# Experts' weights in 2 MB pieces, in places of 16 KB per partition

## The chip, the cores and the metric

The kernel runs on one core of a Trainium2 chip. The metric is the device time of one execution in microseconds (us). Three runs of the kernel before took 2021.32, 2018.51 and 2013.82 us, median 2018.51 us.

## The reference, cut to what matters

Two transformer blocks over 512 tokens of width 1024, all in float32. The first block is a mixer (projections, convolutions, pooling), a LayerNorm, a mixture of experts and a gated side branch ("ple"), then another LayerNorm. The second block has attention, a recurrent part and a dense feed-forward. The change touches the experts:

```
logits = h @ router_w + router_b            # 512 tokens, 32 experts
gates, idx = softmax(top_k(logits, 4))      # every token goes to 4 experts
gu  = x_e @ w_gate_up[e] + b_gate_up[e]     # 1024 -> 2048, tokens of expert e
act = (clip(up) + 1) * min(gate, 7) * sigmoid(1.702 * gate)
y_e = act @ w_down[e] + b_down[e]           # 1024 -> 1024
out[token] += gate * y_e
```

Each of the 32 experts has 8 MB of w_gate_up and 4 MB of w_down, 384 MB in all, and every byte of it is read once.

## The kernel before, in words

The order of the work on each engine is the order of the Python code; a DMA or an instruction waits only for the data it needs and for the space it writes.

The mixer streams its weights through a `Stream`: half-places of 4 KB per partition hold raw weights, ScalarE (line 179) and VectorE (line 188) split each into a high and a low part in the `kh` and `rh` tiles. When the stream is through, these tiles become places for the experts' weights.

The experts run one after the other, 32 of them. Expert 0 is fixed in the code; the order of the others is found at run time, so that 13 "large" ones (up to 96 tokens) and 19 "small" ones (up to 64) alternate: for i = 1 to 6 large, small, large, small, large, small, then large, small, large, small, small over and over. Per step i the code runs `gate_up(i)`, for i = 0, 2, 4, 6 also `gate1` (a quarter of the side branch: 24 matmuls on lines 268 to 270), and then `down(i - 1)`.

Weights come through `Chunks`. A chunk is 1 MB: 128 partitions with 8 KB each. An expert has 8 chunks for `gate_up` and 4 for `down`. The list `free` holds places; `loads` takes the first fitting one and lets SyncE's queue (SP, line 233) issue the DMA into it; `get` hands the next chunk to the matmuls (lines 1137 and 1210); `release(n)` gives the n oldest places back. A small expert releases after each chunk. A large one first runs the matmuls for its first 64 tokens on four chunks, then those for the other 32 tokens on the same four (lines 1143 and 1217), and releases all four then. SP works its queue in order, and at most eight of its DMAs are under way: the ninth waits until the first has landed.

Places before: three chunks are loaded into `rw` tiles ahead of a run-time loop (`overflow`, which runs zero times here but holds all engines until its count is known). After it three places are added (`kh` twice, `zw`), and during expert 0 `kw0`, `kw1` and the last `rw` come free: nine places of 1 MB. At i = 6, when the side branch no longer needs its tiles, nine more are given. The last chunks go only into places that the second block doesn't need early (`tail`, `last`).

GpSimd's queue (POOL) carries the other traffic: per expert a `gather` of its tokens' rows and, in `finish`, a scatter that adds its results to `acc`; in expert 0 also eight accumulating DMAs of 256 KB (`ple_bias`, lines 962 and 968), which read the tiles z0 to z3 and others. `activate(0)` overwrites z0, z1 and z2 (line 1154 is ScalarE's sigmoid into z2), so it waits for the first three of them.

Of the kernel before, what the change touches and what calls it, by code (L numbers as in the profile page):

```python
# [21 lines left out]
T = 512  # L22
D = 1024
# [69 lines left out]
def prepare(i):  # L93
# [25 lines left out]
    o["w_gate_up"] = a["w_gate_up"][0]  # L119
    o["b_gate_up"] = a["b_gate_up"][0]  # L120

    w = a["w_down"][0].reshape(NE, 4, 2, 128, D).transpose(0, 1, 3, 2, 4)
    o["w_down"] = np.ascontiguousarray(w).reshape(NE, 4, 128, 2 * D)
# [89 lines left out]
class Chunks:  # L213


    def __init__(self, nc):
        self.nc, self.free, self.plan, self.raw = nc, [], [], {}
        self.nl = self.pos = 0
        self.limit, self.hold = 0, False
        self.tail, self.last = 0, ()  # L220
# [5 lines left out]
    def loads(self):  # L226
        while not self.hold and self.nl < min(self.limit, len(self.plan)):
            ok = [i for i, (n, p) in enumerate(self.free) if n in self.last or
                  self.nl < len(self.plan) - self.tail * (2 if n[0] == "k" else 1)]
            if not ok:  # L230
                return
            self.raw[self.nl] = place = self.free.pop(ok[0])
            self.nc.sync.dma_start(place[1], self.plan[self.nl]())
            self.nl += 1

    def get(self):
        self.loads()
        self.pos += 1
        return self.raw[self.pos - 1][1]

    def release(self, n):

        for i in sorted(self.raw)[:n]:
            self.free.append(self.raw.pop(i))
        self.loads()
# [3 lines left out]
def kernel(ctx: ExitStack, tc: tile.TileContext, h, out, dbg=None):  # L249
# [47 lines left out]
    kw = [keep.tile([128, 2048], F32, name=f"kw{i}") for i in range(2)]  # L297
    made = {}

    def kh(i, when):  # L300
        if (i, when) not in made:
            made[i, when] = keep.tile([128, 2, 1024], F32R, tag=f"kh{i}", name="kh")
        return two(made[i, when])
# [31 lines left out]
    with ExitStack() as first:  # L335
# [12 lines left out]
        rw_ = [ring.tile([128, 2048], F32, name=f"rw{i}") for i in range(4)]  # L348
        rh = ring.tile([128, 2, 1024], F32R, tag="rh", name="rh")
        whole = {("k", i): w for i, w in enumerate(kw)} | {("r", i): w for i, w in enumerate(rw_)}  # L350
        parts_ = {n: halves(w) for n, w in whole.items()}
        st = Stream(nc, [p for n in (("k", 0), ("r", 0), ("k", 1), ("r", 1), ("r", 2), ("r", 3)) for p in parts_[n]],
                    [L(kh, i, 1) for i in range(5)] + [lambda: two(rh)])
# [16 lines left out]
        xh = [slot(f"s{j}", [128, 4, T], F32R) for j in range(2)]  # L370
        xl = [slot(f"s{2 + j}", [128, 4, T], F32R) for j in range(2)]
# [48 lines left out]
        def plan_gu(i):  # L420
            for k in range(8):
                mo.plan.append(lambda k=k: h["w_gate_up"][expert(i), 128 * k:128 * k + 128].rearrange("a p c -> (a p) c"))

        def plan_d(i):
            for k in range(4):
                mo.plan.append(lambda k=k: h["w_down"][expert(i), k].rearrange("a p c -> (a p) c"))
# [6 lines left out]
        mo.limit = 8  # L433
        mo.tail, mo.last = 8, {("r", i) for i in range(4)} | {"rh", "zw", "s1", "s3"}
        given = set()

        def spare():

            for n, w in whole.items():
                a = halves(w)  # L440
# [256 lines left out]
        hTh = [slot(f"s{j}", [128, 4, T], F32R) for j in range(2)]  # L697
        hTl = [slot(f"s{2 + j}", [128, 4, T], F32R) for j in range(2)]
# [410 lines left out]
        kh_of = lambda i: (f"kh{i}", keep.tile([128, 2048], F32, tag=f"kh{i}", name="kw"))  # L1109
        kh_free = [i for i in range(5) if i not in gates_at]  # L1110
        assert 5 in gates_at and len(kh_free) == 2
# [6 lines left out]
        def gate_up(i, pre={}, post={}):  # L1118
# [10 lines left out]
            w, n0 = [], 4 if b else 1  # L1129
            for c in range(8):  # L1130
# [49 lines left out]
        def turn_act(i):  # L1180
            n = CAP if large(i) else CAPS
            if i < NE - 2:
                AT[i] = t = slot(f"y{6 + i % 2}", [128, 4, 2 * n])
            else:
                AT[i] = t = (zs(3) if i % 2 else slot("s2", [128, 512])).rearrange("p (c s) -> p c s", c=4)
# [11 lines left out]
        def down(i, pre={}, post={}):  # L1197
# [3 lines left out]
            w, n0 = [], 4 if b else 1  # L1201
            for c in range(4):
# [9 lines left out]
                if (c + 1) % n0 == 0:  # L1212
# [6 lines left out]
                    mo.release(n0)  # L1219
# [23 lines left out]
        def overflow():  # L1243
# [3 lines left out]
            with tc.For_i(0, nx, 1) as j:  # L1247
# [23 lines left out]
                s3 = keep.tile([128, 2048], F32, tag=f"kh{kh_free[0]}", name="s3")  # L1271
# [10 lines left out]
                def load_gu(k, c0):  # L1282
                    t = keep.tile([128, 4, 512], F32, tag=f"kh{kh_free[1]}", name="wx")
                    src = h["w_gate_up"][ds(ev, 1)].rearrange("a (k p) c -> p (a k) c", p=128)
                    nc.sync.dma_start(t, src[:, 4 * k:4 * k + 4, c0:c0 + 512])
                    return t

                def load_d(k, c0):
                    t = keep.tile([128, 4, 512], F32, tag=f"kh{kh_free[1]}", name="wx")
                    for q in range(2):  # L1290
                        src = h["w_down"][ds(ev, 1), 2 * k + q].rearrange("a p (j c) -> p (a j) c", j=2)
                        nc.sync.dma_start(t[:, 2 * q:2 * q + 2], src[:, :, c0:c0 + 512])
                    return t
# [3 lines left out]
                for hf in range(2):  # L1297
                    o = [tbank(), tbank()]
                    for g in range(2):
# [3 lines left out]
                        for k in range(8):  # L1303
                            if k % 4 == 0:
                                w = load_gu(k // 4, c0)
                            P.matmul(o[g][:CAP], x32[:, k], w[:, k % 4], start=False, stop=k == 7)
                    turn32(swiglu(o[0][:CAP], o[1][:CAP], z3, gate[-1][:CAP]), a32[:, 4 * hf:4 * hf + 4], 4)
                dn = [tbank(), tbank()]
                for n in range(2):
                    for k in range(8):  # L1310
                        if k % 4 == 0:
                            w = load_d(k // 4, 512 * n)
                        P.matmul(dn[n][:CAP], a32[:, k], w[:, k % 4], start=k == 0, stop=k == 7)
# [7 lines left out]
        mo.limit = 12 * NE  # L1321
        mo.give(*[kh_of(i) for i in kh_free], ("zw", work.tile([128, 2304], F32, tag="zw", name="zw")[:, 0:2048]))
# [23 lines left out]
        for i in range(NE):  # L1346
# [38 lines left out]
        ys = slot("s0", [128, 2, D], F32R)  # L1385
# [601 lines left out]
```

## Time and profile before

| | us |
|---|---|
| median of 3 runs | 2018.51 |
| the profiled execution | 2018.47 |
| its span | 2016.7 |
| TensorE (PE) busy | 1890.4 (94%) |
| VectorE (DVE) busy | 768.8 (38%) |
| ScalarE (ACT) busy | 463.5 (23%) |

The profile is one execution. Times in its views count from the span's start; 1.8 us of the execution lie outside the span. In a row with "x8" eight instructions are merged. The experts run from about 232 to 1319 us; before them lies the mixer, behind them the second block.

### The profile page before, as it was taken

Reading aid. Unit: us, or ns where it says so; the run is one execution under the profiler, and the core shown is the slowest. Engines: PE = TensorE matmul, PEld = TensorE weight load, DVE = VectorE, ACT = ScalarE, POOL = GpSimd, SP = SyncE. Lnnn points to the kernel's source line nnn. Section 1 sums busy time; section 2 is a strip of 40 time slices with the busy share of each in tenths; the row PEclk is TensorE's granted clock in tenths of the full one; section 3 lists DMA queues with packets and bytes.
Section 4 is the critical chain, followed back from the end, with each engine's and each line's share of the span. In section 5 each row is a group of like instructions: output and inputs, shape, how many; then the busy total and the mean of one; then the engine's idle time right before and its main releaser. Section 6 shows DMA issues by size and latency. Waiting matters only on the chain.

```text
span 2016.7 us, 24301 instructions
## 1 busy us (share of the span) xinstructions
PE 1890.4 (94%) x9434; PEld 1063.2 (53%) x9434; DVE 768.8 (38%) x1517; ACT 463.5 (23%) x811; POOL 110.8 (5%) x125
## 2 busy tenths in 40 slices
PE   8999899999998998998998898889999899999998
PEld 7777533333332332332332232258886588888886
DVE  7967721222121221222121111175665653333454
ACT  4333310101010101010101010232226742222342
POOL 0012200000000000000000000100000000000000
PEclk9999899999999999999999999999999899999999
DMA  7225499999999999999999999923220214333331
GB/s 293 83 81 201 172 355 400 396 400 401 392 399 404 399 401 393 408 391 406 396 406 395 407 392 409 379 68 113 63 63 27 74 58 131 94 95 99 100 94 42
DMA packets 97942, 518.17 MB, mean 257 GB/s; under 512 B 11082, under 2 KB 11098, under 8 KB 48544
## 3 DMA queue, kind: packets, MB, share of 16 engines
q1 hardware_dynamic: 85120, 479.17, 61.1%
q0 software_dynamic: 11376, 35.56, 6.6%
q10 hardware_dynamic: 1328, 1.85, 0.3%
q8 instruction: 76, 1.25, 0.2%
q14 instruction: 42, 0.34, 0.1%
HBM read 496.48 MB, written 20.05 MB: 256 GB/s over the span
## 4 chain that ended last, share of the span: by engine, by line
PE 47%; DMA 36%; DVE 3%; ACT 2%; issue 1%; POOL 0%; SPq 0%; DVEq 0%; ACTq 0%
DMA rw<-in_w_gate_up_dram 13%; PE mm L268 9%; PE mm L270 9%; PE mm L269 9%; DMA kw<-in_w_down_dram 7%; PE mm L1137 6%; PE mm L1210 4%; DMA s<-in_w_down_dram 4%; DMA kw<-in_w_gate_up_dram 4%; DMA zz<-in_w_gate_up_dram 4%; DMA s<-in_w_gate_up_dram 3%; PE mm L1143 3%; PE tr L1608 1%; PE tr L1030 1%; DMA acc<-z 1%; PE mm L1217 1%
## 5 line engine op out<-in xcount | busy, mean ns | idle before, releaser
L1137 PE MATMUL mm<-rw,y 128*64 128x512 f32 x768 | 183.3, 602 | 18.0 <-DMA rw<-in_w_gate_up_dram 17.7
L188 DVE TENSOR_TENSOR kh<-kw,kh 128x1024 fp32r<-128x1024 f32 (+1 forms) x116 | 139.4, 1209 | 153.3 <-ACT kh L179 153.1
L1137 PE MATMUL mm<-kw,y 128*64 128x512 f32 x688 | 167.2, 608 | 22.6 <-DMA kw<-in_w_gate_up_dram 22.2
L1154 ACT ACTIVATE z<-z 128x512 f32<-128x512 f32 (+1 forms) x45 | 28.3, 629 | 661.3 <-DVE z L1153 650.4
L179 ACT CAST kh<-kw 128x1024 fp32r<-128x1024 f32 (+1 forms) x116 | 119.9, 1040 | 252.2 <-PE mm L269 170.3
L270 PE MATMUL mm<-vh,kh 128*128 128x512 f32 (+2 forms) x368 | 140.6, 382 | 0.1
L268 PE MATMUL mm<-vh,kh 128*128 128x512 f32 (+2 forms) x368 | 140.6, 382 | 0.0
L269 PE MATMUL mm<-vl,kh 128*128 128x512 f32 (+2 forms) x368 | 140.5, 382 | 0.0
L1193 DVE COPY y<-tr 128x512 f32<-128x512 f32 (+1 forms) x43 | 25.1, 608 | 267.5 <-PE tr L1191 259.0
L1210 PE MATMUL mm<-kw,y 128*64 128x512 f32 x480 | 114.2, 602 | 9.7 <-DMA kw<-in_w_down_dram 9.7
L1137 PEld LDWEIGHTS mm<-rw,y 128*64 128x64 f32 x768 | 50.7, 137 | 127.6 <-issue 83.1
L1137 PEld LDWEIGHTS mm<-kw,y 128*64 128x64 f32 x688 | 43.2, 137 | 114.0 <-issue 67.4
L1153 DVE TENSOR_SCALAR z<-mm 128x512 f32<-128x512 f32 (+1 forms) x45 | 31.2, 693 | 175.2 <-PE mm L1137 158.6
L270 PEld LDWEIGHTS mm<-vh,kh 128*128 128x128 f32 x368 | 69.1, 188 | 13.6 <-DVE kh L188 0.4
L268 PEld LDWEIGHTS mm<-vh,kh 128*128 128x128 f32 x368 | 69.1, 188 | 13.2
L269 PEld LDWEIGHTS mm<-vl,kh 128*128 128x128 f32 x368 | 69.1, 188 | 12.9
L1236 DVE TENSOR_TENSOR y<-mm,z 32x512 f32<-32x512 f32 x26 | 17.8, 683 | 151.5 <-ACT z L1233 151.3
L1137 PE MATMUL mm<-s,y 128*64 128x512 f32 x264 | 63.5, 603 | 10.4 <-DMA s<-in_w_gate_up_dram 10.4
L1210 PEld LDWEIGHTS mm<-kw,y 128*64 128x64 f32 x480 | 30.5, 136 | 76.7 <-issue 46.8
L268 PE MATMUL mm<-kh,uh 128*128 128x512 f32 x160 | 69.2, 433 | 1.0 <-DVE ul L1467 0.7
L1069 POOL DMA_INDIRECT y<-hd,ix x32 | 30.7, 960 | 662.4 <-PE tr L1177 638.8
L1210 PE MATMUL mm<-s,y 128*64 128x512 f32 x256 | 60.2, 601 | 6.2 <-DMA s<-in_w_down_dram 6.2
(540 smaller groups left out, 3214.5 us busy)
## 6 DMA issues: line engine op xcount, KB each, us to landing
rw<-in_w_gate_up_dram SPq DMA_DIRECT2D x96, 1024.0 KB, 21.8
kw<-in_w_gate_up_dram SPq DMA_DIRECT2D x86, 1024.0 KB, 22.1
kw<-in_w_down_dram SPq DMA_DIRECT2D x60, 1024.0 KB, 21.4
s<-in_w_down_dram SPq DMA_DIRECT2D x34, 1024.0 KB, 21.5
s<-in_w_gate_up_dram SPq DMA_DIRECT2D x33, 1024.0 KB, 21.8
rw<-in_w_down_dram SPq DMA_DIRECT2D x31, 1024.0 KB, 22.8
zw<-in_w_gate_up_dram SPq DMA_DIRECT2D x24, 1024.0 KB, 22.4
kw<-in_w_gate_up_dram SPq DMA_DIRECT2D x44, 512.0 KB, 3.5
```

The lines of the kernel that those rows point to most:

```text
L179: self.nc.scalar.copy(hi, t)
L188: self.nc.vector.tensor_tensor(lo, t, hi, op=ALU.subtract)
L268: P.matmul(o, a[0], b[0], start=start, stop=False)
L269: P.matmul(o, a[0], b[1], start=False, stop=False)
L270: P.matmul(o, a[1], b[0], start=False, stop=stop)
L1069: G.indirect_dma_start(out=x[:n], out_offset=None, in_=hd[:, :], in_offset=bass.IndirectOffsetOnAxis(ap=idx[i][:n, 0:1], axis=0))
L1137: P.matmul(o[g][64 * hf:64 * hf + 64], x[:, c, 0:CAPS], w[c][:, c0:c0 + 512], start=False, stop=c == 7)
L1143: P.matmul(o[2][32 * j:32 * j + 32], x[:, k, CAPS:CAP], w[k][:, c0:c0 + 512], start=False, stop=k == 7)
L1153: ts(g, pg, 7.0, None, op0=ALU.min)
L1154: act(out=s, in_=g, func=AF.Sigmoid, scale=1.702)
L1193: V.tensor_copy(d, q[:, 0:4 * m].rearrange("p (c s) -> p c s", c=4))
L1210: P.matmul(o[0][64 * n:64 * n + 64], a[:, q, 64 * hf:64 * hf + 64], w[c][:, c0:c0 + 512], start=k == 0, stop=k == 7)
```

## The change

The host lays out both weights so that a piece of 2 MB is contiguous: 128 partitions with 16 KB, two former chunks side by side. A place now holds 16 KB per partition: `kw0` and `kw1` become one tile, the four `rw` become two, `kh1`/`kh2` and `kh3`/`kh4` are paired, the `s` tiles become `sa` and `sb`. Two pairs that don't lie together (`rh` with `zw`, `kh0` with `zz`) make places that are loaded by two DMAs of 1 MB, as is the very last piece.

`get` still hands out 1 MB (half a piece), so the matmuls and their order don't change. Releases are by piece: a small expert releases after every second chunk, a large one two pieces after every fourth. Two pieces are loaded ahead of the run-time loop. After it one place is added (`kh1` with `kh2`), and `kw` and `rw1` come free during expert 0: four places of 2 MB until i = 6, then nine.

```diff
 class Chunks:
     def loads(self):
...
-            self.raw[self.nl] = place = self.free.pop(ok[0])
-            self.nc.sync.dma_start(place[1], self.plan[self.nl]())
+            n, p = self.free.pop(ok[0])
+            src = self.plan[self.nl]()
...
+            if isinstance(p, tuple) or self.nl == len(self.plan) - 1:
+                for j in range(2):
+                    self.nc.sync.dma_start(half[j], src[:, 2048 * j:2048 * j + 2048])
+            else:
+                self.nc.sync.dma_start(p, src)
...
     def get(self):
...
-        return self.raw[self.pos - 1][1]
+        return self.raw[(self.pos - 1) // 2][1][(self.pos - 1) % 2]
...
-        st = Stream(nc, [p for n in (("k", 0), ("r", 0), ("k", 1), ("r", 1), ("r", 2), ("r", 3)) for p in parts_[n]],
+        ka, ra, rb = [parts_[n] for n in (("k", 0), ("r", 0), ("r", 1))]
+        st = Stream(nc, ka[:1] + rb + ra + ka[1:], [L(kh, i, 1) for i in range(5)] + [lambda: two(rh)])
...
-        mo.limit = 8
-        mo.tail, mo.last = 8, {("r", i) for i in range(4)} | {"rh", "zw", "s1", "s3"}
+        mo.limit = 4
+        mo.tail, mo.last = 4, {("r", 0), ("r", 1), "rz", "sa"}
...
-            w, n0 = [], 4 if b else 1
+            w, n0 = [], 4 if b else 2
...
-                    mo.release(n0)
+                    mo.release(n0 // 2)
...
-        mo.give(*[kh_of(i) for i in kh_free], ("zw", work.tile([128, 2304], F32, tag="zw", name="zw")[:, 0:2048]))
+        mo.give(kp_of(1))
...
             if i == 6:
-                mo.give(*[kh_of(j) for j in range(5) if j in gates_at],
-                        ("rh", ring.tile([128, 2048], F32, tag="rh", name="rw")),
-                        ("zz", new_zz((2304,))[:, 0:2048]),
-                        *[(f"s{j}", slot(f"s{j}", [128, 2048])) for j in range(4)])
+                mo.give(kp_of(2),
+                        ("rz", (ring.tile([128, 2048], F32, tag="rh", name="rw"),
+                                work.tile([128, 2304], F32, tag="zw", name="zw")[:, 0:2048])),
+                        ("kz", (keep.tile([128, 2048], F32, tag="kp0", name="kw"), new_zz((2304,))[:, 0:2048])),
+                        *[(g, slot(g, [128, 4096])) for g in ("sa", "sb")])
```

SP's queue around the run-time loop, before (its count `exi` is read between the second and the third stretch; `kw_1799` and `kw_1800` are the two `kh` places):

```order
L233 DMA rw1_97<-in_w_gate_up_dram 128x2048 [waits DMAHW7_49,DVE_49]
L233 DMA rw2_98<-in_w_gate_up_dram 128x2048 [waits DMAHW0_49,DVE_49]
...
L233 DMA rw3_99<-in_w_gate_up_dram 128x2048 [waits DMAHW1_49,DVE_49]
L1246 TENSOR_LOAD exi_94 [waits DVE_49]
...
L233 DMA kw_1799<-in_w_gate_up_dram 128x2048
L233 DMA kw_1800<-in_w_gate_up_dram 128x2048
L233 DMA zw_1801<-in_w_gate_up_dram 128x2048
L233 DMA rw1_97<-in_w_gate_up_dram 128x2048 [waits PE_49]
L233 DMA rw2_98<-in_w_gate_up_dram 128x2048 [waits PE_49]
```

The same place now (`kw_76` is the one tile of `kw`, `kw_1781` the pair of `kh1` and `kh2`):

```order
L243 DMA rw0_95<-in_w_gate_up_dram 128x4096 [waits DMAHW7_49,DVE_49,Activation_49]
...
L243 DMA kw_76<-in_w_gate_up_dram 128x4096 [waits DMAHW0_49,DVE_49]
L1263 TENSOR_LOAD exi_93 [waits DVE_49]
...
L243 DMA kw_1781<-in_w_gate_up_dram 128x4096
L243 DMA rw0_95<-in_w_gate_up_dram 128x4096 [waits PE_49]
```

Four former chunks instead of three stand ahead of the loop; behind it one DMA (two former chunks) instead of three waits for nothing, and the next needs matmuls to end.

SP's queue a little later, the end of expert 0's `gate_up`, expert 1's `gate_up` (large) and expert 0's `down`, before:

```order
L233 DMA kw0_76<-in_w_gate_up_dram 128x2048 [waits DVE_49]
...
L233 DMA rw3_99<-in_w_gate_up_dram 128x2048 [waits PE_49]
...
L233 DMA kw_1799<-in_w_gate_up_dram 128x2048 [waits DMAHW6_49,PE_49]
...
L233 DMA rw0_96<-in_w_gate_up_dram 128x2048 [waits DVE_49]
...
L233 DMA kw_1800<-in_w_gate_up_dram 128x2048 [waits DMAHW7_49,PE_49]
...
L233 DMA rw1_97<-in_w_gate_up_dram 128x2048 [waits DMAHW2_49,PE_49]
L233 DMA rw2_98<-in_w_down_dram 128x2048 [waits DMAHW3_49,PE_49]
L233 DMA kw0_76<-in_w_down_dram 128x2048 [waits DMAHW4_49,PE_49]
L233 DMA rw3_99<-in_w_down_dram 128x2048 [waits DMAHW5_49,PE_49]
```

And now:

```order
L243 DMA kw_76<-in_w_gate_up_dram 128x4096 [waits PE_49]
...
L243 DMA rw1_96<-in_w_gate_up_dram 128x4096 [waits DVE_49]
...
L243 DMA kw_1781<-in_w_gate_up_dram 128x4096 [waits DMAHW1_49,PE_49]
...
L243 DMA rw0_95<-in_w_gate_up_dram 128x4096 [waits DMAHW2_49,PE_49]
L243 DMA kw_76<-in_w_down_dram 128x4096 [waits DMAHW3_49,PE_49]
L243 DMA rw1_96<-in_w_down_dram 128x4096 [waits DMAHW4_49,PE_49]
```

Expert 1's `gate_up` fills all four places (`kw_76`, `rw1_96`, `kw_1781`, `rw0_95`); expert 0's `down` goes into the first two again, which expert 1's matmuls release together. Before, nine places were in turn, and the DMAs of `down` go into other tiles than those of the same group.

## Rows read from the trace of the kernel before

**Rows 1.** The page, section 2: busy tenths in 40 slices, DMA and GB/s.
```profile
DMA  7225499999999999999999999923220214333331
GB/s 293 83 81 201 172 355 400 396 400 401 392 399 404 399 401 393 408 391 406 396 406 395 407 392 409 379 68 113 63 63 27 74 58 131 94 95 99 100 94 42
```
**Rows 2.** Busy by stretch: length, PE, PEld, DVE, ACT, POOL, clock, DMA share, GB/s.
```profile
357.60:425.20 67.60, 67.16 (x378) 26.19 (x374) 15.23 (x34) 7.68 (x15) 5.80 (x5) 1.00 1.02 395
500.00:1262.00 762.00, 694.47 (x3720) 232.87 (x3720) 152.26 (x337) 77.36 (x152) 54.56 (x46) 1.00 1.02 400
```
**Rows 3.** SP's timeline, 1208 to 1260 us: start, length, what it issued.
```profile
1246.82 0.33 SPq L233 DMA_DIRECT2D zw<-in_w_gate_up_dram  x1
...
1256.76 0.33 SPq L233 DMA_DIRECT2D zz<-in_w_gate_up_dram  x1
```
**Rows 4.** SP's waits, 290 to 470 us: total, times, longest.
```profile
SPq L233 <- PE mm L1143: 40.0, 14, 9.3
SPq L233 <- PE mm L1217: 36.9, 10, 11.6
```
**Rows 5.** DMA queue of SP, 24 to 30 us: packets, MB, share of 16 engines.
```profile
q1 hardware_dynamic: 678, 2.49, 101.9%
```
**Rows 6.** The same queue, 1241 to 1259 us.
```profile
q1 hardware_dynamic: 1041, 7.60, 100.7%
```
**Rows 7.** SP's timeline, 225 to 262 us.
```profile
231.65 0.94 SPq L233 DMA_DIRECT2D kw<-in_w_gate_up_dram  x2
```
**Rows 8.** PE's timeline, 196 to 256 us, expert 0.
```profile
237.49 1.94 PE L1137 MATMUL mm<-rw,y 128*64 128x512 f32 x8
```
**Rows 9.** The page, section 6: times issued, KB each, us from issue to landing.
```profile
kw<-in_w_gate_up_dram SPq DMA_DIRECT2D x44, 512.0 KB, 3.5
```
**Rows 10.** The chain that ended last, 225 to 300 us: start, us, what.
```profile
243.74 1.18 POOL acc L962 x2
244.91 15.76 DMA acc<-z
...
260.76 0.04 ACT z L1154
...
261.88 0.38 ACT y L1178
...
262.30 5.37 PE mm L1137 x24
```
**Rows 11.** DMA queues, 248 to 272 us: packets, MB, share of 16 engines.
```profile
DMA packets 1804, 8.26 MB, mean 344 GB/s; under 512 B 194, under 2 KB 194, under 8 KB 996
...
q1 hardware_dynamic: 906, 6.62, 68.4%
q0 software_dynamic: 898, 1.64, 37.0%
```
**Rows 12.** PE's timeline, 330 to 405 us, experts 3 and 4.
```profile
335.87 1.94 PE L1137 MATMUL mm<-zw,y 128*64 128x512 f32 x8
...
346.23 1.04 PE L1143 MATMUL mm<-kw,y 128*32 128x512 f32 x8
...
358.84 1.04 PE L1143 MATMUL mm<-kw,y 128*32 128x512 f32 x8
...
368.29 1.94 PE L1137 MATMUL mm<-kw,y 128*64 128x512 f32 x8
...
403.45 1.94 PE L1137 MATMUL mm<-rw,y 128*64 128x512 f32 x8
```
**Rows 13.** PE's timeline, 465 to 475 us, start of expert 7.
```profile
471.54 1.94 PE L1137 MATMUL mm<-kw,y 128*64 128x512 f32 x8
```
**Rows 14.** The chain that ended last, 1255 to 1340 us.
```profile
1287.26 1.94 PE mm L1210 x8
1289.20 7.07 PE tr L1341 x12
...
1317.31 1.89 PE mm L1210 x8
```

More of the change, by code (lines that the diff above doesn't have):

```diff
@@ L231, in loads @@
                 return
-            self.raw[self.nl] = place = self.free.pop(ok[0])
-            self.nc.sync.dma_start(place[1], self.plan[self.nl]())
+            n, p = self.free.pop(ok[0])
+            src = self.plan[self.nl]()
+            half = [x[:, 2048 * j:2048 * j + 2048] for x in ([p] if not isinstance(p, tuple) else []) for j in range(2)]
+            half = half or list(p)
+            if isinstance(p, tuple) or self.nl == len(self.plan) - 1:
[3 more added lines that the diff above has]
+                self.nc.sync.dma_start(p, src)
+            self.raw[self.nl] = ((n, p), half)
             self.nl += 1
@@ L295 @@
     act(out=eps2, in_=eps[:, 0:1], func=AF.Sigmoid)
-    kw = [keep.tile([128, 2048], F32, name=f"kw{i}") for i in range(2)]
+    kwt = keep.tile([128, 4096], F32, name="kw")
+    kw = [kwt[:, 0:2048], kwt[:, 2048:4096]]
     made = {}
     def kh(i, when):
-        if (i, when) not in made:
-            made[i, when] = keep.tile([128, 2, 1024], F32R, tag=f"kh{i}", name="kh")
-        return two(made[i, when])
+        j = (i + 1) // 2
+        if (j, when) not in made:
+            made[j, when] = keep.tile([128, 4 if j else 2, 1024], F32R, tag=f"kp{j}", name="kh")
+        t = made[j, when]
+        return two(t[:, 2 - 2 * (i % 2):4 - 2 * (i % 2)] if j else t)
     halves = lambda w: [w[:, 1024 * i:1024 * i + 1024] for i in range(2)]
@@ L367, in zs, with eight @@
             return work.tile([128, 576], dt, tag=f"z{i}", name=f"z{i}")[:p, :n]
-        xh = [slot(f"s{j}", [128, 4, T], F32R) for j in range(2)]
-        xl = [slot(f"s{2 + j}", [128, 4, T], F32R) for j in range(2)]
+        def eight(tag):
+            t = slot(tag, [128, 8, T], F32R)
+            return [t[:, 0:4], t[:, 4:8]]
+        xh, xl = eight("sa"), eight("sb")
         flat = lambda t: t.rearrange("p a b -> p (a b)")
@@ L420, in plan_gu @@
         def plan_gu(i):
-            for k in range(8):
-                mo.plan.append(lambda k=k: h["w_gate_up"][expert(i), 128 * k:128 * k + 128].rearrange("a p c -> (a p) c"))
+            for k in range(4):
+                mo.plan.append(lambda k=k: h["w_gate_up"][expert(i), k].rearrange("a p c -> (a p) c"))
         def plan_d(i):
-            for k in range(4):
+            for k in range(2):
                 mo.plan.append(lambda k=k: h["w_down"][expert(i), k].rearrange("a p c -> (a p) c"))
@@ L696 @@
             resid(t, 0, o0[t])
-        hTh = [slot(f"s{j}", [128, 4, T], F32R) for j in range(2)]
-        hTl = [slot(f"s{2 + j}", [128, 4, T], F32R) for j in range(2)]
+        hTh, hTl = eight("sa"), eight("sb")
         bns = lambda t: tiny[:, 32 + 16 * t:32 + 16 * t + 16]
@@ L1108 @@
         gates_at = {(st.nh + j) % 6 for j in range(4)}
-        kh_of = lambda i: (f"kh{i}", keep.tile([128, 2048], F32, tag=f"kh{i}", name="kw"))
-        kh_free = [i for i in range(5) if i not in gates_at]
-        assert 5 in gates_at and len(kh_free) == 2
+        assert gates_at == {3, 4, 5, 0}
+        kp_of = lambda j: (f"kp{j}", keep.tile([128, 4096], F32, tag=f"kp{j}", name="kw"))
         show("posm", posm)
@@ L1282, in load_gu @@
                 def load_gu(k, c0):
[L1283 to L1286, printed above, removed]
+                    for q in range(2):
+                        src = h["w_gate_up"][ds(ev, 1), 2 * k + q].rearrange("a p (j c) -> p (a j) c", j=2)
+                        nc.sync.dma_start(wx[:, 2 * q:2 * q + 2], src[:, :, c0:c0 + 512])
                 def load_d(k, c0):
[L1289 to L1293, printed above, removed]
+                    src = h["w_down"][ds(ev, 1), k].rearrange("a p (j c) -> p (a j) c", j=4)
+                    nc.sync.dma_start(wx, src[:, :, c0:c0 + 512])
                 turn32(xr, x32, 8)
```

38 lines of the change are left out of this document (19 added, 19 removed).

## The prediction

> **What bounds the kernel now.** I read the page first. From slice 7 to 25 of 40 the DMA stands at 9 tenths and near 400 GB/s [rows 1]: the experts, 384 MB of weights. By stretches, the DMA is never idle there (share 1.02; packets overlap a little), while PE is busy 67.16 of 67.60 us early and 694.47 of 762 us later [rows 2]. So from about 500 us on only the DMA counts, and before that DMA and PE are level: a delay of either is kept. In the quiet, SP issues a chunk of 1 MB every (1256.76 - 1246.82) / 4 = 2.485 us [rows 3], each when an older one has landed, since eight are under way. Early it waits for matmuls instead: 24 waits on the two lines that end a large expert's group, 76.9 us in 180 [rows 4]. There the number of places decides, not the count of DMAs under way.
>
> The end is fixed by the DMA until the second-last expert's `down`: after the wait that ends at 1287.26 PE runs its own work to 1317.31 [rows 14].
>
> **Longer pieces.** The change makes 16 KB pieces out of 8 KB ones. How a piece's length pays, two stretches with full queues show: with 4 KB pieces the queue moved 2.49 MB in 6 us at a share of 101.9% [rows 5], 407 GB/s of its own time; with 8 KB pieces 7.60 MB in 18 us at 100.7% [rows 6], 419 GB/s. Halving the count of pieces gave 2.9%; if that is a fixed cost per piece, the next halving gives half of it, 425 GB/s: a million-byte MB (1.0486 million bytes) in 2.465 instead of 2.501 us, 0.036 us saved. The ends: nothing saved, if the piece isn't what costs, or as much again as the last step, 0.071 us. I take 0.036, the value that a fixed cost gives; a loss I leave out, since the longer piece was the faster one in the rows.
>
> The Trainium skill (DMA: Bandwidth & Descriptors, "Where 436 GB/s comes from") puts the fabric's ceiling at 435 GB/s; by that page a MB can't fall under 2.41 us, at most 0.09 saved, and no run here shows the ceiling.
>
> Where does this pay? Where the DMA alone decides, behind i = 6. By the code PE has then used 7 x 8 + 6 x 4 = 80 MB, and at most four pieces are ahead: about 300 MB are left. Seven of nine places take 16 KB pieces, the two pairs still 8 KB ones: 233 MB x 0.036 = 8.4 us saved (0 to 16.5).
>
> **The start.** Ahead of the run-time loop four MB are loaded instead of three, worth 2.5 us of DMA. Behind it, three chunks were issued at once from 231.65 on [rows 7]; now one piece of 4.9 us, and the next waits until expert 0's second chunk is used, at 239.4 [rows 8]. From issue to landing a lone 512 KB takes 3.5 us [rows 9], of which 1.3 is transfer at 407 GB/s: 2.2 us pass before data flows. The lone piece ends at 231.65 + 2.2 + 4.9 = 238.8 and the next starts at 241.6: 2.8 us idle, against 2.5 gained. Nothing, then; and PE has its weights in time, so expert 0's matmuls hide it.
>
> **The turn-taking with POOL's queue.** Between 243.74 and 262.30 the chain runs over an accumulating DMA from z, then ScalarE's L1154, which overwrites z2, and behind it in ScalarE's queue the copy L1178, for which PE's first matmul of expert 1 waits [rows 10]. In that stretch 1804 packets ran, 194 of them only completions, 802 of POOL's 2 KB and 808 of SP's 8 KB [rows 11]: one for one. Per engine that is 50.5 such pairs in 24 us, 0.475 us each: 0.31 for SP's piece (2.485 / 8), 0.165 for POOL's. An accumulate of 256 KB is 8 pieces per engine: 3.8 us. If one for one holds with 16 KB pieces, a turn lasts 0.61 + 0.165 = 0.775, the accumulate 6.2 us, and the third of them, for which L1154 waits, comes 3 x 2.4 = 7.2 us later. Behind L1154 are ScalarE's work for the side branch and L1178, and PE waits for the latter, with everything behind it. The ends: 0, if the engines switch within a piece, and 9, if the `gather` ahead (96 rows of 4 KB, six per engine) is delayed by 6 x 0.3 too. I take 7.2, what one for one gives.
>
> The Trainium skill (DMA: Bandwidth & Descriptors, "Queues, rings and completion order") says that an engine goes round its queues packet by packet, a packet being typically 9 to 17 descriptors. The rows agree with the turns but not with that length, since SP's 8 KB pieces each get a turn; by the page's length a turn would hold a whole chunk and the three accumulates would have taken some 60 us, against 15.8 for the chain's piece. The measurement decides.
>
> **Four places of 2 MB until i = 6.** A pair of experts (large, small) took 335.87 to 403.45, 67.6 us [rows 12], the one before it 262.30 to 335.87 [rows 10, 12], the next 403.45 to 471.54 [rows 12, 13]: 209.2 for the three. Its 24 chunks need 59.6 us of DMA, so the rest of the queue's time, 8.0 us, is POOL's traffic. Nine places kept five filling while four were held by a large group of 11.4 to 12.6 us (335.87 to 347.3 to 359.9 [rows 12]): five chunks last 12.4 us, and the queue never ran dry. Now a group holds two places, and the other two fill in 9.8 us. Counting from the large `gate_up`: its first group ends at 11.4; if both other places are full by then, the two pieces of the small `down` start at 13.6 and end at 23.5; the next places come free at 24.0, and data flows again at 26.2: 2.7 us idle. The small `gate_up`'s first two pieces land at 31.1 and 37 (a `gather` between them), the second wanted at 36; a scatter makes the third land at 44, wanted at 42, and the fourth is 0.6 late. After the large `down` the same gap of 2.7 comes once more. So PE loses about 4 us a pair: 67.6 + 3.9 = 71.5, three pairs 214.5, 5.3 more than before (the first pair, at 73.6, was slow already). The ends: no gap at all, 67.2 a pair (PE's own 67.16), 7.6 less than before; or a gap at all three joint releases, 59.2 + 8.0 + 3 x 2.7 = 75.3, 16.7 more. I take the timetable's.
>
> **The tail.** The second-last expert's first half-piece can be used only when 2 MB have landed, 3.8 us later beside POOL's loads; but SP's share in the turns grows, 3.1 instead of 3.8 us per MB over the last five chunks, which gives 3.5 back. 0.5 us lost (0 to 3.8); the last piece is split, and PE's 30 us [rows 14] cover what follows.
>
> The second block and the mixer keep their instructions and their order on PE, ACT and DVE. I cost this at nothing: the paired `kh` tiles are written half by half, as the `kw` halves were.
>
> **Sum**, from the profiled execution (2018.47, span 2016.7, the median 2018.51): + 7.2 + 5.3 + 0.5 - 8.4 = + 4.6, 2023 us. What one can tell from no change is about 0.5%, 10 us.
>
> **Rivals.**
> *The queue runs dry at every joint release* (slower). It is one mechanism, the four places until i = 6: it decides when the two free places are filled before the group ends. For it: SP's 24 early waits on just those lines [rows 4]. Against it: POOL's 8 us a pair lie in some of the gaps. 16.7 instead of 5.3: 2034 us.
> *Pieces of 16 KB save nothing*, because the engine cuts them or the cost isn't per piece; the change then only makes places coarser. For it: no row shows a piece over 8 KB. Against it: the step from 4 to 8 KB. + 13.0: 2031.5 us.
> *The turns don't lengthen*: engines switch within a piece. For it: nothing but that 16 KB was never seen; against it the count of packets [rows 11]. - 2.6: 2016 us.
> *Full gain* (faster): the turns stay and no gap opens, so that - 7.6 + 0.5 - 8.4 = - 15.5: 2003 us. For it: DMA and PE are so level that 1.5% less DMA could free both; against it the timetable.
>
> **Chances.** Forecast 0.42 (its own range 2015 to 2030), dry queue 0.16, nothing saved 0.14, turns as before 0.14, full gain 0.14. The range to be right 8 times in 10 reaches to the slow cases and leaves out most of the full gain: 2008 to 2036. Faster by over 0.5%: nearly all of the full gain and little else, 0.14. Slower: the two slow cases, less a part of the second, and a little of the forecast, 0.29. The same: 0.57.
>
> **What would show it.** Per piece: the quiet interval between SP's issues or landings at 4.9 us per 2 MB (4.97: nothing saved), and between 600 and 1200 us a period of 12 MB shorter by 0.3 to 0.4 us. Turns: expert 1's first matmul near 269.5 instead of 262.30, with ScalarE's L1154 waiting for acc<-z some 18 us. Places: pairs of 71 to 72 us, a DMA share under 1.0 between 290 and 480, PE waiting for the small expert's `gate_up`. Hand-over: expert 7 near 484. Wrong would be a start of expert 7 before 475, or a gain behind it over 16 us or none.

## The result, and the profile after

Four runs of the changed kernel took 2027.68 to 2031.63 us, median 2029.55; before in the same comparison 2019.84. The ratio is 1.0058 (95%: 1.0046 to 1.0069): slower by about 10 us (the two medians differ by 9.7), inside the range, 6.5 us above the 2023 that was forecast. The profiled execution was the slowest of the four, 2031.63 us (span 2029.8), 13.1 us of span more than before.

The starts of some experts, read from PE's timeline (the first matmul on `btab`, line 1141, before 1124), show where these 13.1 us are:

| stretch, us | before | after | difference |
|---|---|---|---|
| start of the span to expert 0 | 231.54 | 232.27 | +0.7 |
| expert 0 to 1 | 29.44 | 29.53 | +0.1 |
| expert 1 to 3 | 73.77 | 79.60 | +5.8 |
| expert 3 to 7 | 135.67 | 144.29 | +8.6 |
| expert 7 to 8 | 32.87 | 32.88 | 0.0 |
| expert 8 to 31 | 761.33 | 760.88 | -0.4 |
| expert 31 to the end | 752.1 | 750.4 | -1.7 |

So all the loss lies before expert 8, and the 8.4 us that longer pieces were to give back behind i = 6 didn't come.

The page after, section 2, the lines that answer to [rows 1]:

```profile
DMA  8225499999999999999999999923220113333331
GB/s 296 77 85 217 159 332 382 389 358 379 397 404 388 409 391 408 399 411 391 409 393 400 406 399 404 402 75 114 63 63 27 64 62 125 103 95 94 100 98 42
```

Slices 7 to 10 moved 382, 389, 358 and 379 GB/s where before moved 400, 396, 400 and 401. From slice 11 on the two lines are much alike.

Busy by stretch after, the columns of [rows 2]:

```profile
290.00:357.60 67.60, 64.13 (x358) 24.79 (x354) 14.71 (x29) 7.69 (x15) 5.82 (x5) 1.00 0.97 374
357.60:425.20 67.60, 64.25 (x351) 23.86 (x352) 15.21 (x33) 7.59 (x15) 5.81 (x5) 1.00 0.98 378
425.20:500.00 74.80, 71.94 (x378) 27.62 (x374) 15.21 (x33) 7.69 (x15) 5.80 (x5) 0.95 0.94 368
500.00:1262.00 762.00, 701.73 (x3762) 244.82 (x3762) 156.51 (x349) 76.87 (x150) 54.64 (x46) 0.98 1.01 401
```

The DMA has gaps now until 500 us (share 0.94 to 0.98), and PE waits as well. Behind 500 the DMA is never idle, but it moves 401 GB/s, before 400 [rows 2].

The chain that ended last, after, 225 to 310 us, and PE's timeline there (in brackets the idle time before and what ended it), against [rows 10]:

```profile
244.54 1.18 POOL acc L980 x2
245.72 22.13 DMA acc<-z
...
268.47 0.58 ACT z L997
269.05 0.38 ACT y L1195
269.47 7.39 PE mm L1154 x24
```

```profile
269.47 5.67 PE L1154 MATMUL mm<-kw,y 128*64 128x512 f32 x16 [6.51 <-ACT y L1195]
```

The accumulating DMA took 22.13 us instead of 15.76, and PE's first matmul of expert 1 starts at 269.47 instead of 262.30. The queues in the same 24 us as in [rows 11]:

```profile
q1 hardware_dynamic: 532, 7.83, 78.4%
q0 software_dynamic: 625, 1.15, 26.2%
```

POOL's queue moved 1.15 MB instead of 1.64, SP's 7.83 instead of 6.62.

In the quiet stretches SP issues a piece of 2 MB every 4.90 us, against 2 x 2.485 [rows 3]; SP's timeline after, 730 to 750 us:

```profile
737.79 0.33 SPq L243 DMA_DIRECT2D sa<-in_w_down_dram  x1
742.69 0.33 SPq L243 DMA_DIRECT2D sb<-in_w_down_dram  x1
747.58 0.33 SPq L243 DMA_DIRECT2D kw<-in_w_gate_up_dram  x1
```

So the 0.036 us per MB are there between these issues (4.97 - 4.90 = 0.07 for two), and over the whole stretch they are not.

### The profile page after: what moved, and what is told of

Read it like the earlier page. It is cut to its first block, busy times and chain, and to the rows that moved or that the text cites. A ratio compares the mean times of both kernels' runs of the same rounds, so it can differ in the third digit from the quotient of the medians.

```text
span 2029.8 us, 23685 instructions
## 1 busy us (share of the span) xinstructions
PE 1900.3 (94%) x9434; PEld 1075.4 (53%) x9434; DVE 768.8 (38%) x1517; ACT 463.5 (23%) x811; POOL 110.9 (5%) x125
## 4 chain that ended last, share of the span: by engine, by line
PE 43%; DMA 40%; DVE 3%; ACT 2%; issue 1%; POOL 0%; DVEq 0%; SPq 0%; ACTq 0%; POOLq 0%
DMA kw<-in_w_gate_up_dram 17%; PE mm L280 9%; PE mm L282 9%; PE mm L281 9%; DMA kw<-in_w_down_dram 8%; PE mm L1154 5%; PE mm L1227 4%; DMA sb<-in_w_gate_up_dram 3%; DMA rw<-in_w_gate_up_dram 2%; PE mm L1160 2%; DMA sa<-in_w_gate_up_dram 2%; DMA rw<-in_w_down_dram 2%; DMA sa<-in_w_down_dram 2%; DMA sb<-in_w_down_dram 2%; DMA rest<-acc 1%; PE tr L1623 1%
## 5 line engine op out<-in xcount | busy, mean ns | idle before, releaser
L1154 PE MATMUL mm<-kw,y 128*64 128x512 f32 x864 | 211.6, 620 | 27.3 <-DMA kw<-in_w_gate_up_dram 20.7
L1154 PE MATMUL mm<-rw,y 128*64 128x512 f32 x712 | 168.1, 606 | 12.6 <-DMA rw<-in_w_gate_up_dram 11.7
L1154 PEld LDWEIGHTS mm<-kw,y 128*64 128x64 f32 x864 | 57.2, 140 | 145.3 <-issue 99.2
L1227 PE MATMUL mm<-kw,y 128*64 128x512 f32 x352 | 80.4, 598 | 6.2 <-DMA kw<-in_w_down_dram 6.2
L282 PEld LDWEIGHTS mm<-vh,kh 128*128 128x128 f32 x368 | 69.1, 188 | 13.5 <-DVE kh L190 0.5
L281 PEld LDWEIGHTS mm<-vl,kh 128*128 128x128 f32 x368 | 69.1, 188 | 13.1
L1227 PE MATMUL mm<-rw,y 128*64 128x512 f32 x288 | 66.6, 599 | 4.4 <-DMA rw<-in_w_down_dram 4.4
L280 PE MATMUL mm<-kh,uh 128*128 128x512 f32 x160 | 68.9, 431 | 1.4 <-DVE ul L1482 1.2
L282 PE MATMUL mm<-kh,ul 128*128 128x512 f32 x160 | 63.9, 400 | 0.5 <-DVE ul L1482 0.5
L281 PE MATMUL mm<-kh,uh 128*128 128x512 f32 x160 | 63.8, 398 | 0.0
```

The costliest lines, as they stand in the source:

```text
L280: P.matmul(o, a[0], b[0], start=start, stop=False)
L281: P.matmul(o, a[0], b[1], start=False, stop=False)
L282: P.matmul(o, a[1], b[0], start=False, stop=stop)
L1154: P.matmul(o[g][64 * hf:64 * hf + 64], x[:, c, 0:CAPS], w[c][:, c0:c0 + 512], start=False, stop=c == 7)
L1227: P.matmul(o[0][64 * n:64 * n + 64], a[:, q, 64 * hf:64 * hf + 64], w[c][:, c0:c0 + 512], start=k == 0, stop=k == 7)
```

## The experiments

Theory at first: the pieces of 16 KB cost 7.2 us at POOL's turns and, through coarse places, the rest of the early loss, and give nothing back later. The rivals: the gain behind i = 6 is real but coarser places eat it there; the early loss is places alone. Numbers of all kernels stand in a table behind the runs.

**Halves everywhere.** Places and releases as changed, each piece as two DMAs:

```diff
-            if isinstance(p, tuple) or self.nl == len(self.plan) - 1:
+            if True:
```

> The changed kernel, its places and releases kept, but every piece of 2 MB loaded by two DMAs of 1 MB (128 x 8 KB). Theory 1 (pieces of 16 KB cost 7.2 us at POOL's turns in expert 0 and give nothing back behind i = 6): ScalarE's copy before expert 1 and PE's first matmul of expert 1 come back from 269.5 to about 262.5 us, expert 8 starts near 511.5 instead of 518.6, the stretch from expert 8's start to expert 31's stays at 761 us, and the median falls from 2029.5 to about 2022.5. Theory 2 (the longer pieces do save their 7 to 8 us behind i = 6, and coarser places lose as much there): the start comes back as well, but the stretch from expert 8 to 31 grows to 768 and the median stays near 2030. Theory 3 (the early loss is places alone): expert 1 still starts near 269.

Median 2019.56 us, ratio to before 1.0003 (0.999 to 1.0015): all of the loss is gone, more than theory 1 said, for the stretch from expert 3 to 7 came back as well (136.63 us). So four places of 2 MB and releases by two chunks cost nothing that these runs show, as long as each half is loaded by a DMA of its own, which waits for its own half of the place alone. The chain shows the old turns:

```profile
242.90 15.77 DMA acc<-z
```

Expert 8 to 31 took 762.69 us, 1.8 more than with 16 KB: theory 2 (768) falls.

**Halves until i = 6.**

```diff
-            if isinstance(p, tuple) or self.nl == len(self.plan) - 1:
+            if self.halves or isinstance(p, tuple) or self.nl == len(self.plan) - 1:
...
             if i == 6:
+                mo.halves = False
```

> The changed kernel with pieces as two DMAs of 8 KB per partition until i = 6, and as one of 16 KB behind it. The start of expert 1 near 262.5 and of expert 8 near 511.5, as in the kernel with halves everywhere; the stretch from expert 8 to expert 31 at 761, median 2022.5, by theories 1 and 2 alike. Against the kernel with halves everywhere this is the worth of 16 KB pieces where the DMA alone decides: theory 1 says under 1.5 us between the two, theory 2 says 7 to 8.

Median 2019.47, ratio 1.0008 (0.9998 to 1.0017), 0.1 us from the kernel with halves everywhere. Whatever pieces of 16 KB behind i = 6 are worth, it is less than these intervals can show (some 3 us).

**ScalarE's wait taken away.** `activate(0)` writes into tiles that no accumulating DMA reads:

```diff
-            acts[i] = [swiglu(o[0], o[1], [zs(j) for j in range(3)], gate[i])]
+            z = [zs(j) for j in range(3)]
+            if i == 0:
+                t = work.tile([128, 4, 576], F32, tag="zw", name="zw")
+                z = [t[:, j, :512] for j in range(3)]
+            acts[i] = [swiglu(o[0], o[1], z, gate[i])]
```

> The changed kernel with one edit: activate(0) writes its three tiles into the tile zw, which is unused at that time, instead of z0 to z2, which the accumulating DMAs read. Pieces stay at 16 KB. Theory 1 (the lengthened turns hurt only through ScalarE's wait for z2): ScalarE's copy and expert 1's first matmul come 6.5 to 7 us earlier, near 263, and about as much is left at the end: median about 2023. Rival (the DMA is what is late, PE's wait only covers it): expert 1 starts near 263, but waits for its weights then, expert 8 starts at 518 as before the edit, and the median stays near 2029.5.

Median 2032.59, ratio 1.0071 (1.0057 to 1.0086). Expert 1's matmuls start at 260.74, as wanted, and nothing is won. Not the weights come late then, as the rival had it, but the next thing on POOL's queue. POOL's timeline and PE's in this kernel:

```profile
275.75 0.98 POOL L1087 DMA_INDIRECT y<-hd,ix  x1 [0.30 <-issue]
```

```profile
301.55 1.09 PE L1198 MATMUL tr<-cst,y 64*128 64x64 f32 x8 [13.21 <-DMA y<-hd,ix]
```

The gather of expert 2's rows, issued at 275.75 behind the eight accumulating DMAs, is late now, and PE waits 13.21 us for it; the chain puts 25.66 us down to this DMA. Expert 3 starts at 341.66, before this edit at 341.40, although expert 0 began 2.1 us sooner here. ScalarE's wait was only the first place where the stretched queue showed.

**Long DMAs of short pieces.** The weights lie in DRAM as before (two chunks, one behind the other), so that one DMA of 2 MB has 256 pieces of 8 KB:

```diff
-    w = a["w_gate_up"][0].reshape(NE, 4, 2, 128, 2 * D).transpose(0, 1, 3, 2, 4)
-    o["w_gate_up"] = np.ascontiguousarray(w).reshape(NE, 4, 128, 4 * D)
+    o["w_gate_up"] = a["w_gate_up"][0].reshape(NE, 4, 2, 128, 2 * D)
...
-                self.nc.sync.dma_start(p, src)
+                self.nc.sync.dma_start(p.rearrange("p (j c) -> p j c", j=2), src)
```

> The changed kernel with its places and its one DMA of 2 MB per piece, but both weights lie in DRAM as in two chunks per piece, so that each DMA moves 256 pieces of 8 KB instead of 128 of 16 KB. It parts the length of a piece from the size of a DMA. Theory 3 (two prices: pieces of 16 KB stretch POOL's queue in expert 0; a DMA of 2 MB into one place costs the pairs of experts 3 to 7, since it must wait for both halves of its place and lands as a whole): PE's first matmul behind ScalarE's copy for expert 1 comes back to 260 to 262.5, the start of expert 3 to 332 to 335, and the stretch from expert 3 to expert 7 stays at 144 us (changed kernel 144.3, with halves 136.6); median about 2027. Rival 4 (the length of a piece costs in both places, since gathers and scatters come late beside it): 136 to 138 us from expert 3 to 7, median about 2019.5.

Median 2028.53, ratio 1.0048 (1.0035 to 1.0061). Most of the loss is there without any piece of 16 KB. POOL's queue has its turns back, 248 to 272 us:

```profile
q1 hardware_dynamic: 867, 6.71, 69.1%
q0 software_dynamic: 867, 1.58, 35.6%
```

Expert 1 isn't late (first matmul at 258.92), expert 3 starts at 333.94 (expert 0 began 3.3 us sooner than before the change), and the stretch from 3 to 7 takes 141.88 us, 2 less than theory 3 said. Theory 3 stands, rival 4 (136 to 138) falls.

**Halves for the first 13 pieces only.**

```diff
-            if isinstance(p, tuple) or self.nl == len(self.plan) - 1:
+            if self.nl < 13 or isinstance(p, tuple) or self.nl == len(self.plan) - 1:
```

> The changed kernel with only the first 13 pieces loaded as two DMAs of 8 KB per partition (those issued up to about 300 us, beside POOL's accumulating DMAs), all later ones as one of 16 KB. Theory 3: expert 1 and expert 3 start as with halves everywhere (expert 3 at 332 to 335), then 144 us from expert 3 to expert 7; median about 2027. Rival 5 (one price: only the start is lost, and the pairs are slow only because they begin in another phase): 136 to 138 us from expert 3 to 7, median about 2019.5.

Median 2025.14, ratio 1.0034 (1.0022 to 1.0045). Expert 3 starts at 336.22, a little later than expected, and 3 to 7 takes 142.08 us: the pairs lose without a late start too, and rival 5 falls.

**Waiting for the whole place, landing by halves.** The piece is cut at column 2112 of 4096:

```diff
+                for a, b in ((0, 2112), (2112, 4096)):
+                    self.nc.sync.dma_start(p[:, a:b], src[:, a:b])
```

> The changed kernel with every piece loaded by two DMAs, cut not in the middle but at column 2112 of 4096: the first carries 64 columns of the second half, so it must wait until both halves of its place are free (as the one DMA of 2 MB does), but it lands by itself, after 1.03 MB, and PE can use the first half then. Pieces are 8.4 and 7.9 KB, so that expert 0's turns should be those of the kernel with halves (PE's first matmul of expert 1 near 262). Theory 3a (what costs the pairs is the wait for both halves of a place): 141.5 to 143 us from expert 3 to expert 7, median near 2026. Theory 3b (what costs is that a piece lands as a whole, 2.4 us later for its first half): 136.5 to 138 us, median near 2019.5. Both alike: between, near 139.5.

Median 2020.04, ratio 1.0009 (1.0 to 1.0018), 138.41 us from expert 3 to 7. Busy by stretch from expert 3 to 7, in this order: before, halves everywhere, this kernel, the long DMAs of short pieces, and the changed kernel:

```profile
334.75:470.42 135.67, 134.47 (x745) 52.25 (x741) 30.42 (x66) 15.37 (x30) 11.61 (x10) 1.00 1.02 396
```

```profile
332.04:468.67 136.63, 134.81 (x745) 52.07 (x741) 30.41 (x66) 15.38 (x30) 11.62 (x10) 1.00 1.01 391
```

```profile
333.60:472.01 138.41, 135.09 (x744) 52.01 (x740) 30.42 (x66) 15.37 (x30) 11.61 (x10) 1.00 1.01 387
```

```profile
333.94:475.82 141.88, 135.13 (x745) 52.00 (x741) 30.41 (x66) 15.37 (x30) 11.61 (x10) 1.00 0.99 377
```

```profile
341.40:485.69 144.29, 138.09 (x744) 53.35 (x740) 30.42 (x66) 15.28 (x30) 11.62 (x10) 0.98 0.96 372
```

From halves to whole DMAs the stretch grows by 5.25 us; the wait for both halves of a place makes 1.8 of it, and 3.5 come with landing as a whole. With halves, in this kernel and with the long DMAs PE is idle for 1.8, 3.3 and 6.75 us, and the DMA moves 391, 387 and 377 GB/s. The likely way is that PE can't begin on the first half until the second has landed, so it uses and frees its places later, and the queue runs dry; what else differs between one DMA and two isn't separated. Each stretch is one execution. Other kernels repeat them closely at a clock of 1.00 (halves until i = 6 took 136.66 us, whole DMAs 141.98, next), but the medians don't tell the two landings (1.0009) from halves everywhere (1.0003).

The changed kernel's 2.4 us more, in which PE is busier, not idler, at a clock of 0.98, are not shown to come from the length of its pieces. Three kernels of the next experiment (at 16 KB: without POOL's late traffic, with the gathers alone, with both) are the changed kernel up to expert 8. There the same stretch took 142.24, 143.27 and 141.98 us, the last at a clock of 1.00 (its row is below); in their three partners, the changed kernel up to i = 6, it took 141.45 to 144.43.

```profile
337.94:479.92 141.98, 135.04 (x745) 52.01 (x741) 30.40 (x66) 15.28 (x30) 11.61 (x10) 1.00 0.98 378
```

**Where the gain behind i = 6 went.** One question, six kernels: does a piece of 16 KB pay when SP's queue is alone, and what is left of it beside POOL's? Two kernels without POOL's late traffic (the matmuls left out in `down` in the same way; where pieces are 8 KB, they are loaded in halves behind i = 6):

```diff
+            if i > 9:
+                X[i] = X[i - 1]
+                return
...
+            if i > 7:
+                return
             G.indirect_dma_start(out=acc[:, :], out_offset=bass.IndirectOffsetOnAxis(ap=idx[i][:n, 0:1], axis=0),
...
-                        for k in range(c + 1 - n0, c + 1):
+                        for k in range(c + 1 - n0, c + 1) if i < 8 else [7][:c // 7]:
```

> The changed kernel; behind expert 8 it leaves out POOL's gathers and scatters (experts 10 and on reuse expert 9's rows, results from expert 8 on are not added) and most of the matmuls for a large expert's other 32 tokens, so that PE is well under the DMA (about 620 us in 23 experts). From expert 10 on only SP's queue loads, 16 KB pieces in seven of nine places. Theory 1a (16 KB pieces save 0.035 us per MB by themselves, and turns with POOL's traffic take it back): about 29.5 us per expert; from the start of expert 12 to that of expert 30, 18 experts, 530.8 us. Theory 1b (the saving is not there in the mean): 536.8 us, 12 x 2.485 per expert.

> The same, POOL's late traffic and most of a large expert's other matmuls left out, but with two DMAs of 8 KB per partition for every piece behind i = 6. Both theories: 18 experts in about 536.8 us; against the kernel with 16 KB pieces 6 us longer by theory 1a, the same by 1b.

Two with all of POOL's traffic and the same lightened PE:

> The changed kernel with POOL's traffic kept; only most of the matmuls for a large expert's other 32 tokens are left out from expert 8 on, so that PE is no longer near the DMA. Theory 1a and 1b (the DMA alone decides, PE is not what took the gain): expert 12 to expert 30 as in the changed kernel, within 2 us. Theory 2 (large experts' late releases took the gain): 5 to 6 us shorter than in the changed kernel.

> The same light kernel, POOL's traffic kept, with two DMAs of 8 KB per piece behind i = 6. Theory 1a and 1b: expert 12 to expert 30 within 1.5 us of the light kernel with 16 KB pieces. Theory 2: 5 to 6 us longer than it.

And two with the gathers, but not the scatters:

> The light kernel (most of a large expert's other matmuls left out behind expert 8), with POOL's gathers kept and its accumulating scatters left out from expert 8 on. 16 KB pieces. From the start of expert 12 to that of expert 30 it was 536.8 us with neither and 596.9 with both. Theory 1a (every POOL packet takes back a little of the saving, whichever kind): halves cost about 3 us more in this stretch, 565 to 570 us here. Theory 1c (only the scatters take it back, gathers don't): halves cost 4.6 us more, as without POOL's traffic.

> The same with two DMAs of 8 KB per piece behind i = 6: expert 12 to expert 30 was 541.4 us without POOL's late traffic and 598.4 with all of it. Theory 1a: about 3 us longer than with 16 KB pieces; theory 1c: 4.6 us longer.

Busy by stretch from expert 12 to 30 (the last number is GB/s). Without POOL's traffic, 16 KB, then 8 KB:

```profile
630.65:1167.42 536.77, 489.31 (x2402) 176.73 (x2400) 122.37 (x272) 60.52 (x119) 4.60 (x7) 0.98 1.01 426
```

```profile
629.04:1170.43 541.39, 494.59 (x2402) 165.47 (x2400) 122.33 (x272) 60.56 (x119) 4.60 (x7) 1.00 1.01 421
```

With the gathers, 16 KB, then 8 KB:

```profile
640.34:1213.60 573.26, 495.35 (x2403) 177.91 (x2401) 123.16 (x272) 60.53 (x119) 19.29 (x23) 0.97 1.01 407
```

```profile
637.49:1211.05 573.56, 502.14 (x2402) 166.68 (x2400) 122.45 (x272) 60.56 (x119) 19.83 (x23) 0.99 1.01 407
```

With gathers and scatters, the light kernels:

```profile
639.64:1236.55 596.91, 506.94 (x2403) 180.22 (x2401) 122.68 (x272) 60.59 (x119) 42.93 (x36) 0.95 1.01 400
```

```profile
640.60:1239.00 598.40, 508.87 (x2402) 168.66 (x2400) 122.66 (x272) 60.52 (x119) 43.14 (x36) 0.98 1.02 400
```

The changed kernel and the one before:

```profile
646.76:1244.88 598.12, 549.74 (x2963) 191.35 (x2961) 122.38 (x272) 60.57 (x119) 42.77 (x36) 0.98 1.01 401
```

```profile
630.65:1230.37 599.72, 547.91 (x2962) 184.67 (x2961) 122.35 (x272) 60.51 (x119) 42.71 (x36) 1.00 1.02 400
```

Alone, 16 KB save 4.6 us in 18 experts (theory 1a said 6); beside the gathers 0.3, beside both 1.5. With PE busy 506.94 us instead of 549.74, the light kernel gains 1.2 us over the changed kernel, not 5 to 6, so it isn't late releases of large experts (theory 2). Theory 1c, that only scatters take it back, falls; 1a is right that the traffic takes it back, but not in its share for the gathers, 3 us, nor in its time beside them (573.26 us for 565 to 570). Each of these is one execution. In the heavy kernels the same stretch took 598.12 to 600.27 us with 16 KB behind i = 6 (four kernels) and 599.72 to 600.59 with about 8 KB (four): so 0.3 and 1.5 are not told apart, while 4.6 is outside that spread.

The queue's own row shows it per byte. DMA queues over those stretches, alone and with gathers, at 16 KB (packets, MB, share of 16 engines):

```profile
q1 hardware_dynamic: 19129, 228.05, 100.5%
```

```profile
q1 hardware_dynamic: 19072, 227.34, 97.5%
q0 software_dynamic: 1664, 5.64, 3.1%
```

The same at 8 KB:

```profile
q1 hardware_dynamic: 31231, 227.44, 101.1%
```

```profile
q1 hardware_dynamic: 31236, 227.48, 97.9%
q0 software_dynamic: 1664, 5.64, 3.3%
```

At 16 KB, alone, 100.5% of 536.77 us for 228.05 MB is 2.366 us of queue time per million bytes; beside the gathers 97.5% of 573.26 for 227.34 is 2.459. For 8 KB it is 2.407 and 2.468. The gathers stretch the long pieces by 0.093 and the short ones by 0.062, and of a lead of 0.041 there remains 0.010. Why a longer piece is stretched more, no run here shows.

**All kernels.**

| kernel | median, us | ratio to before | expert 1 to 3 | 3 to 7 | 8 to 31 |
|---|---|---|---|---|---|
| before | 2019.84 | | 73.77 | 135.67 | 761.33 |
| changed | 2029.55 | 1.0058 | 79.60 | 144.29 | 760.88 |
| halves everywhere | 2019.56 | 1.0003 | 73.08 | 136.63 | 762.69 |
| halves until i = 6 | 2019.47 | 1.0008 | 72.65 | 136.66 | 761.95 |
| wait taken away | 2032.59 | 1.0071 | 82.02 | 144.39 | 761.61 |
| long DMAs, 8 KB | 2028.53 | 1.0048 | 76.12 | 141.88 | 761.31 |
| halves first | 2025.14 | 1.0034 | 76.99 | 142.08 | 761.54 |
| whole place, two landings | 2020.04 | 1.0009 | 74.10 | 138.41 | 762.06 |

Each ratio is to runs of the kernel before in the same comparison (their medians lay between 2017.21 and 2019.84 us), so it isn't the quotient with the first row.

Of the changed kernel's early loss (14.5 us from expert 0 to expert 8, halves 0.2), the long DMAs alone make 8.7, the length of the pieces the other 5.9, in single executions. In the three other executions of the same opening the loss was 11.0, 11.8 and 13.5 us, so the length makes 2.4 to 5.9. In the medians the share of the length is smaller: 1.0058 against 1.0048, with intervals that overlap. No kernel of these beats the one before.

## Why the prediction was right or wrong

**What bounds the kernel.** Right. A delay before expert 8 was kept to the end: 14.5 us of it at expert 8, 14.1 at expert 31, beside a start 0.7 later.

**The start.** Right: the queue had gaps, but PE's expert 0 took 29.53 us, before 29.44.

**The turns, + 7.2.** The mechanism and the place are right: expert 1 at 269.47 for 269.5, ScalarE's wait for z2 17.24 us for "some 18", and with 8 KB pieces the turns and the start come back. That expert 1 fits so closely is luck: 0.7 us of its delay is a later start of expert 0, the accumulating DMA grew by 6.4 us, and in the three other executions of the same opening it grew by 4.4 to 5.9 (20.19 to 21.63 us), with expert 1 at 265.59 to 266.06. But this isn't what the length cost: ScalarE's wait could be taken away without gain. The price is POOL's queue as a whole, accumulates and then the gather behind them. What takes a turn is the piece, not the DMA: a DMA of 2 MB with 8 KB pieces left POOL its share (867 packets each in 24 us), one with 16 KB pieces did not. The Trainium skill (DMA: Bandwidth & Descriptors, "Queues, rings and completion order") has the engines change queues by packets of typically 9 to 17 descriptors; no run here shows turns of that length. The prediction's 60 us for such turns was a wrong sum: an accumulate, too, is only eight pieces per engine, so turns of a whole chunk would also have given the equal counts of [rows 11]. What speaks against them is the long DMA of short pieces, with 16 pieces per engine: the counts stayed equal there.

**Four places, + 5.3.** The pairs did lose, and the places are not the cause. The three pairs took 217.35 us (269.47 to 486.82) for 214.5, so the loss was 8.1 for 5.3; in the three other executions they took 215.25 to 218.16. The timetable counted the joint releases of large experts; halves in the same four places, with the same releases in the code, take 209.5 (before 209.2). That a piece is usable only when all of it has landed, which the timetable held too, is the larger part (3.5 of the 5.25 from expert 3 to 7). The Trainium skill (Perfetto Trace Analysis, "DMA Optimizations") says both that larger DMAs use the memory better and that splitting them may let some work start sooner where the DMA engines are idle; by the runs only the second counted in these pairs (138.41 against 141.88 us), though the gaps were small (share 0.99). Of the profiled execution's 8.6 us from expert 3 to 7 a part is PE's clock, which the timetable didn't have (below). And the two prices, turns and pairs, are no plain sum: the first pair took 73.05 us behind the late start, 76.14 with the long DMAs, where expert 1 is on time.

**Longer pieces, - 8.4.** This is the step that failed. The number per MB was right between single issues in the quiet: 4.90 us per 2 MB. Over 18 experts with SP's queue alone it was 0.027 (4.6 us for the 168 MB in pieces of 16 KB), and beside POOL's traffic nothing that can be told from the spread of single executions (0.09 us per expert, 598.12 against 599.72 us in 18 experts, for the 0.3 to 0.4 that was forecast). The mistake was to multiply the quiet number by all of 233 MB, as if POOL's traffic took a fixed time of its own beside it. Measured - 0.4 in all, and by the prediction's own sign ("a gain behind it over 16 us or none") this is where it was wrong. The rival "pieces of 16 KB save nothing" forecast about this time, 2031.5, for another reason: the cost is per piece, but POOL's traffic stretches a longer piece more.

**The tail, + 0.5.** Measured - 1.7 from expert 31 on in the profiled execution, but that stretch holds the whole second block. To the end of expert 31's `down` it was 52.1 us for 54.6 before; over all kernels here this part takes 52 to 59 us, so one execution doesn't weigh a term of 0.5. There is a new wait in it. The chain after, 1280 to 1345 us:

```profile
1282.34 10.51 DMA acc<-y,ix
1292.90 0.51 issue
1293.40 25.83 DMA rest<-acc
1319.28 1.98 PE mm L1427 x4
...
1329.68 1.89 PE mm L1227 x8
```

Before, PE's own work stood there [rows 14]; now the last scatter and POOL's loads of `acc` end last. PE waited 1.27 us for them, so PE's 30 us did not quite cover what follows.

The rivals "turns don't lengthen" and "full gain" are out by the chain and by the gaps. "The queue runs dry" came near in size (2034, its gaps are there), but halves in four places show that the joint releases don't decide it.

**The sum.** That the time lies in the range is in part luck. The range of 2008 to 2036 also held two rivals, 2031.5 and 2034. The early loss of 7.2 + 5.3 came out near the 11.0 to 14.5 measured, but it was put down to ScalarE's wait and to the places, and the experiments clear both. The gain of 8.4 that was to be set against it didn't come.

## What to carry to other kernels

A price per piece that was read in a stretch where one queue is alone holds for that stretch; where a second queue mixes in, read it there, from bytes and share of the whole stretch. When two transfers are merged into one, ask first what becomes usable later, then what must be free earlier, and only then what the longer piece saves: here the landing as a whole cost more than the wait for a whole place (3.5 and 1.8 us, in single executions), and both more than the saving. And a wait that a slow queue causes is not removed by freeing its first victim; look at what is next in that queue.

## What the runs showed that was not expected

A piece of 16 KB beside POOL's gathers costs more per byte than alone by 0.093 us per million bytes, one of 8 KB by 0.062, which all but levels them (above).

Short waits of PE can cost more than their length. In the changed kernel PE waited 0.73 us at 450.16 and 2.13 us before 457.07; the granted clock then fell. PE's timeline and the stretches around it (the clock is the number before DMA share and GB/s):

```profile
450.16 1.94 PE L1154 MATMUL mm<-rw,y 128*64 128x512 f32 x8 [0.73 <-DMA rw<-in_w_gate_up_dram]
...
453.00 1.94 PE L1154 MATMUL mm<-rw,y 128*64 128x512 f32 x8
457.07 2.91 PE L1154 MATMUL mm<-kw,y 128*64 128x512 f32 x8 [2.13 <-DMA kw<-in_w_gate_up_dram]
...
461.71 3.41 PE L1154 MATMUL mm<-kw,y 128*64 128x512 f32 x8
```

```profile
455.00:460.00 5.00, 2.93 (x9) 0.68 (x9) 0.00 (x0) 0.00 (x0) 0.00 (x0) 0.79 1.04 430
460.00:465.00 5.00, 5.00 (x18) 2.74 (x20) 0.44 (x3) 0.00 (x0) 0.00 (x0) 0.53 0.99 426
465.00:470.00 5.00, 5.00 (x25) 2.20 (x22) 2.05 (x3) 0.63 (x1) 0.00 (x0) 1.00 1.00 429
```

Eight matmuls took 3.41 us instead of 1.94, near the lower of the two levels (0.53 of 2.4 GHz; 1.2 GHz would be 0.50), and then the clock was back. A wait of that length doesn't always do it. One of 2.04 us in the same execution left the matmuls behind it at 1.94 us:

```profile
386.72 1.94 PE L1154 MATMUL mm<-kw,y 128*64 128x512 f32 x8 [2.04 <-DMA kw<-in_w_gate_up_dram]
```

Over the whole stretch from expert 3 to 7 PE was busy 138.09 us for the 134.47 of before, the same work; in the three other executions of the same opening 135.04 at a clock of 1.00, and 136.36 and 136.72 at 0.99.
